# Up-projection of a two-layer-norm encoder trunk: a product form with four weight sums, accumulating PSUM banks and moved right-hand pools

## The chip, the cores and the metric

The kernel runs on one core of a Trainium2 chip. Its time is the device time of one execution in microseconds (us). The work is done by five engines that run side by side, each through its own queue of instructions in order: TensorE (PE, matrix products), VectorE (DVE), ScalarE (ACT), GpSimd (POOL) and SyncE (SP, which here only issues DMAs). Products are summed in PSUM, in eight banks of 512 fp32 columns per partition; all other tiles are in SBUF.

## What is computed

One layer with two sub-layers: token mixing (two attention branches and their merge) and a gated MLP with a causal convolution. The change touches the second, and the places where the first hands over to it:

```python
x = _layer_norm(alpha * x + (1.0 + g1) * mix, ln1_g[l], ln1_b[l])

h = _layer_norm(x) * (1.0 + sc2) + sh2
u = _causal_depthwise_conv(h @ w_up[l], conv_w[l], conv_b[l])   # width 3
a, val = jnp.split(u, 2, axis=-1)
y = (jax.nn.silu(a) * val) @ w_down[l]
x = _layer_norm(alpha * x + (1.0 + g2) * y, ln2_g[l], ln2_b[l])
```

S = 1024 rows, D_MODEL = 1024, D_FF = 2816; `h @ w_up` is 1024x1024 by 1024x5632.

## The kernel before

**Operands.** Every fp32 operand of a large product is split into a rounded high part and the rest (`hi`, `lo`, both fp32r), and a product of two is made of three matmuls: high by high, high by low, low by high (`mm3`). A "product" in the up-projection (`product`, L733) is 128 output channels by 512 rows with 512 of the contracted columns: 4 steps of k by 3 matmuls, 12 matmuls of 128x128 by 128x512, into one PSUM bank of the pool `mxp` (6 banks, tag "mm").

**Seven products for eight.** The 2816 gate channels a and the 2816 value channels go in 22 blocks c of 128. For one c the four weight parts are b12, b22 (value) and b11, b21 (gate), each 512x128, and h is cut into four parts h11, h12, h21, h22 of 512 by 512. Strassen's form takes seven products with sums of weights (`operand`, L723: an optional sum on DVE or POOL, a cast by ACT for the high part, a subtraction on POOL or DVE for the low part) and sums of h that are made once: `h_11`, `h_11p12` in the pool `ha` (left-hand side of SBUF) and `h_11p22`, `h_21p22`, `h_21m11`, `h_22`, `h_12m22` in the pool `hb` (right-hand side; tiles named hc0 to hc4 in the program). Each product has a bank of its own; ACT copies (L990, L992, L998) and eight DVE sums (L994 to L1007) join them in the single pair u of convolution inputs (uv the value half, ua the gate half). `conv` (L961) then runs on a PSUM tile `pcv`: ACT Identity (L963), two DVE multiply-adds (L965), and for the gate also silu on ACT (L968) and the product with the value half on DVE (L969). The result goes to DRAM.

**Order.** For c < 8 two of the seven products (of `h_11` and `h_11p12`) are made ahead (`ready`, `head`) and kept in DRAM (`md`): the heads 0 to 2 beside the second layer norm, 3 to 7 beside `turned_1`. The up-projection then alternates early blocks (five products left) with full ones: 0, 8, 1, 9, ... 7, 15, 16 ... 21. `raw` brings weights from DRAM by SP, 512 KB per half block; `slot` gives out ten tiles in turn for split weights.

**Stages, by time in the profile.** Attention until about 715 us; the merge of row half 0 (`merge`, products `psb` and then the mix `psm`) to 825; of half 1 beside the norms of half 0 to 872; `turned_0` (transposes h of half 0 and makes its operands) and the second mix to 959, with heads 0 to 2; `turned_1` (operands of half 1) with the heads 3 to 7 and the spreading of the row g2 (`psrow`) to 1007; the up-projection to 1392; the down-projection to the end. `put` (L867) makes one operand of h: an optional sum (L872), the high part (L874), the low part (L875), on three engines given by the call.

**Placement.** The pools `edge` (an unused tile, 32 bytes per partition), `wide`, the merge operands `oh`/`ol` and `hb` are on the right-hand side, so the size of `edge` sets where the others start.

## Time and profile before

| | |
|---|---|
| runs, us | 1648.75, 1640.61, 1645.29 |
| median, us | 1645.29 |
| the profiled execution's own time, us | 1646.35 |
| its span, first to last instruction, us | 1644.6 |
| mean granted TensorE clock | 0.981 of full |
| PE busy | 1566.4 us, 95% |
| DVE, ACT, POOL busy | 1144.6, 781.2, 560.1 us |

The span is what the trace shows; 1.75 us of the execution lie around it. A stage table (busy time of each engine in a stretch) tells which engine fills a stage, a list by line and shape gives counts and mean durations, and the timeline gives starts, from which the distance of two matmuls is read: a matmul's own duration overlaps the next.

### The profile page before, as it was taken

How to read it: one execution, taken by the hardware profiler on the slowest of the kernel's cores; microseconds unless marked ns; L12 is line 12 of the kernel's file. 1: busy time of each engine (PE TensorE's matmuls, PEld its weight loads, DVE VectorE, ACT ScalarE, POOL GpSimd, SP SyncE). 2: the span in 40 equal slices, each digit the busy share in tenths (PEclk: the TensorE clock that was granted, in tenths of full speed). 3: DMA queues.
4: the chain of work that ended last, by engine and by line, in shares of the span. 5: the costliest groups of instructions: out<-in, count | busy, mean ns of one | idle time of the engine just before them, and what ended most of it. 6: DMA issues, size and time to landing. Idle time of an engine off the chain costs nothing.

```text
span 1644.6 us, 22113 instructions
## 1 busy us (share of the span) xinstructions
PE 1566.4 (95%) x7821; PEld 1300.7 (79%) x7821; DVE 1144.6 (70%) x2293; ACT 781.2 (48%) x1382; POOL 560.1 (34%) x522
## 2 busy tenths in 40 slices
PE   6899999989999999999997979999999999999996
PEld 3787888879888888877875757888888888888885
DVE  6748776686677665537599786999998776544617
ACT  3447555655565556654235264544444444431311
POOL 1111213112222322222063756554455443650602
PEclk9999999999999999999998998999999999999998
DMA  9123432342152334246546244333322222851611
GB/s 346 45 85 121 145 92 70 120 129 65 65 179 78 103 103 123 71 150 236 166 154 230 96 166 160 115 110 122 129 102 90 77 71 90 270 197 39 204 39 52
DMA packets 81823, 205.81 MB, mean 125 GB/s; under 512 B 8560, under 2 KB 17328, under 8 KB 81712
## 3 DMA queue, kind: packets, MB, share of 16 engines
q1 hardware_dynamic: 77104, 197.49, 36.6%
q10 hardware_dynamic: 4608, 6.90, 1.1%
q8 instruction: 62, 1.02, 0.3%
q14 instruction: 49, 0.40, 0.1%
HBM read 157.14 MB, written 38.83 MB: 119 GB/s over the span
## 4 chain that ended last, share of the span: by engine, by line
PE 77%; DVE 13%; DMA 4%; ACT 2%; issue 2%; POOL 2%; DVEq 0%; SPq 0%; ACTq 0%; POOLq 0%
PE psu L213 8%; PE psu L212 8%; PE psu L211 8%; PE psd L1035 5%; PE psd L1033 5%; PE psd L1034 4%; PE pso L509 4%; PE psg L211 4%; PE psg L212 4%; PE psg L213 3%; PE pst L494 3%; PE psq L212 3%; PE psq L211 3%; PE psq L213 3%; PE psv L306 2%; PE psv L305 2%
## 5 line engine op out<-in xcount | busy, mean ns | idle before, releaser
L98 POOL TENSOR_TENSOR wl<-ws,wh 128x1024 fp32r<-128x1024 f32 x54 | 133.1, 2468 | 316.0 <-ACT wh L97 265.3
L1027 DVE TENSOR_TENSOR gl<-gs,gh 128x512 fp32r<-128x512 f32 x41 | 62.3, 1524 | 104.9 <-ACT gh L1026 100.2
L1033 PE MATMUL psd<-dd,gh 128*128 128x512 f32 x328 | 127.6, 389 | 0.0
L1034 PE MATMUL psd<-dd,gh 128*128 128x512 f32 x328 | 127.6, 389 | 0.0
L1035 PE MATMUL psd<-dd,gl 128*128 128x512 f32 x328 | 127.4, 389 | 0.0
L459 ACT ACTIVATE s<-s,mx 128x640 f32<-128x640 f32 (+7 forms) x128 | 94.6, 739 | 48.4 <-DVE mx L453 46.9
L498 ACT CAST pt<-pst 128x512 fp32r<-128x512 f32 (+1 forms) x192 | 82.4, 452 | 67.3 <-PE pst L494 63.4
L211 PE MATMUL psq<-h1h,wh 128*128 128x512 f32 x256 | 104.5, 410 | 0.4 <-DVE h1h L207 0.4
L211 PE MATMUL psu<-hc,wx 128*128 128x512 f32 x264 | 104.0, 394 | 0.0
L212 PE MATMUL psu<-hc,wx 128*128 128x512 f32 x264 | 104.0, 394 | 0.0
L213 PE MATMUL psu<-hc,wx 128*128 128x512 f32 x264 | 104.0, 394 | 0.0
L211 PE MATMUL psg<-h1h,wh 128*128 128x512 f32 x256 | 103.9, 406 | 0.0
L212 PE MATMUL psq<-h1l,wh 128*128 128x512 f32 x256 | 101.1, 395 | 1.8 <-DVE h1l L208 1.8
L213 PE MATMUL psq<-h1h,wl 128*128 128x512 f32 x256 | 101.0, 394 | 0.0
L499 DVE TENSOR_TENSOR pt<-pst,pt 128x512 fp32r<-128x512 f32 (+1 forms) x192 | 96.8, 518 | 5.9 <-ACT pt L498 4.0
L212 PE MATMUL psg<-h1l,wh 128*128 128x512 f32 x256 | 100.2, 392 | 0.0
L213 PE MATMUL psg<-h1h,wl 128*128 128x512 f32 x256 | 100.2, 391 | 0.0
L509 PE MATMUL pso<-pt,vs 128*128 128x256 f32 x608 | 92.1, 290 | 3.1 <-DVE o L514 1.7
L965 DVE SCALAR_TENSOR_TENSOR pcv<-u,convp,pcv 128x1024 f32<-128x1024 f32 x66 | 84.9, 1287 | 13.5 <-ACT pcv L963 12.6
L1021 POOL TENSOR_TENSOR dd<-ws,dd 128x1024 fp32r<-128x1024 f32 x25 | 62.2, 2490 | 89.1 <-ACT dd L1020 89.0
L509 PEld LDWEIGHTS pso<-pt,vs 128*128 128x128 f32 x608 | 81.8, 191 | 12.5 <-ACT pt L498 4.0
L963 ACT ACTIVATE pcv<-u,convp 128x1024 f32<-128x1024 f32 x44 | 53.2, 1210 | 76.0 <-DVE u L1007 31.4
(282 smaller groups left out, 4536.0 us busy)
## 6 DMA issues: line engine op xcount, KB each, us to landing
ws<-in_w_up SPq DMA_DIRECT2D x52, 512.0 KB, 3.7
wa<-in_w_ada SPq DMA_DIRECT2D x64, 256.0 KB, 3.0
ws<-in_w_down SPq DMA_DIRECT2D x28, 512.0 KB, 3.5
yd<-y SPq DMA_DIRECT2D x22, 512.0 KB, 2.6
gs<-yd SPq DMA_DIRECT2D x44, 256.0 KB, 3.7
wa<-in_w_ada SPq DMA_DIRECT2D x8, 1024.0 KB, 12.1
ws<-in_w_qk SPq DMA_DIRECT2D x16, 512.0 KB, 4.7
ws<-in_w_g SPq DMA_DIRECT2D x16, 512.0 KB, 3.8
```

Source lines behind the costliest of these rows:

```text
L98: po.tensor_sub(out=lo, in0=st, in1=hi)
L211: pe.matmul(ps, wh, xh, start=start, stop=False)
L212: pe.matmul(ps, wh, xl, start=False, stop=False)
L213: pe.matmul(ps, wl, xh, start=False, stop=stop)
L459: se.activation(out=st[:, 0:nk], in_=st[:, 0:nk], func=AF.Exp, scale=-1.0, bias=prev, accum_out=sm)
L498: se.copy(out=dh, in_=src)
L499: ve.tensor_sub(out=dl, in0=src, in1=dh)
L509: pe.matmul(ps[:, 0:256], vs[:, j0 + j, :], pt[c][j // 4][:, j % 4, :], start=j == 0 and c == 0, stop=j == nj - 1 and c == 1)
L965: ve.scalar_tensor_tensor(out=ps if d == 1 or b == 0 else y, in0=u[b][:, 2 - d : S + 2 - d], scalar=cp[:, 2 - d : 3 - d], in1=ps, op0=ALU. ...
L1033: pe.matmul(ps[n], g[0][:, ts], d[0][:, halves(n)], start=start, stop=False)
L1034: pe.matmul(ps[n], g[0][:, ts], d[1][:, halves(n)], start=False, stop=False)
L1035: pe.matmul(ps[n], g[1][:, ts], d[0][:, halves(n)], start=False, stop=stop)
```

## The change

The up-projection takes another seven-product form. Two sums follow from one another, s1 = w21 + w22 and s2 = s1 - w11, and two more are w12 - s2 and w11 - w21 (w11, w12 are the gate's parts, w21, w22 the value's); of h it takes h_11 and h_21 as they are (left-hand pool), and h_22, t1 = x - h11, t2 = y - t1, t3 = y - x, t4 = h21 - t2 (right-hand pool), where in the code x and y are the two column halves of the second row half. Products that end in the same output are added in PSUM: `main` takes w11 by h_11, then s2 by t2, (w11 - w21) by t3 and w22 by t4 on top of one another, `side` takes s1 by t1 and then (w12 - s2) by h_22; between two such products the bank is read off by an ACT copy or by a DVE sum. A sum of two such readings is all that is left of the joining. The number of products and of matmuls is the same. All low parts of the up-projection's weights are made on POOL. There are two pairs u in turn, the gate half is convolved first, and silu writes the SBUF tile y that the value half is multiplied into.

The heads are now w11 by h_11 and w12 by h_21, without a sum of weights; the second is added to the first by DVE instead of copied by ACT. `turned_0` casts h_21 without a sum. The unused tile `edge` grows from 32 to 96 bytes per partition, and in the built program every operand of the right-hand pools starts 64 bytes lower (modulo 128 bytes: before at 0, after at 64; the operand tiles of the left-hand pools are at 64 in both). The scratch for dynamic DMA shrinks from 16384 to 1024 bytes.

```diff
...
     edge = ctx.enter_context(tc.tile_pool(name="edge", bufs=1, side="right"))
-    po.memset(edge.tile([P, 8], F32, name="edge", tag="edge"), 0.0)
+    po.memset(edge.tile([P, 24], F32, name="edge", tag="edge"), 0.0)
 
...
     ha_cm, hap = opened(name="ha", bufs=1)
-    h_11, h_11p12 = operands(hap, "ha"), operands(hap, "hb")
+    h_11, h_21 = operands(hap, "ha"), operands(hap, "hb")
     mxp = ctx.enter_context(tc.tile_pool(name="mxp", bufs=6, space=PSUM, reuse_waits="tile"))
...
         if y is not None:
-            t = tmp.tile([P, 4, P], F32, name=nm("wt"), tag="ht", bufs=2 if tmp is mxb else 3)
+            t = tmp.tile([P, 4, P], F32, name=nm("wt"), tag="ht", bufs=2 if tmp is mxb else 4)
             eng.tensor_tensor(out=t, in0=x, in1=y, op=op)
...
 
-    def product(w, h):
-        ps = mxp.tile([P, H], F32, name=nm("psu"), tag="mm")
+    def product(w, h, ps=None):
+        on = ps is not None
+        if not on:
+            ps = mxp.tile([P, H], F32, name=nm("psu"), tag="mm")
         for k in range(4):
-            mm3(ps, w[:, 0, k, :], w[:, 1, k, :], h[k][0], h[k][1], k == 0, k == 3)
+            for a_, b_ in ((0, 0), (0, 1), (1, 0)):
+                first = k == 0 and (a_, b_) == (0, 0) and not on
+                pe.matmul(ps, w[:, a_, k, :], h[k][b_], start=first, stop=k == 3 and a_ == 1, skip_group_check=on)
         return ps
...
         if c < HEAD:
-            b12, b22 = raw(c, 1, wp, "ws")
+            w11, w12 = raw(c, 0, wp, "ws")
             raws.clear()
             lo = ve if c >= EARLY else po
-            readied.append((operand(head_slot, mxb, b12, b22, ALU.subtract, po, lo), operand(head_slot, mxb, b22, lo=lo)))
+            readied.append((operand(head_slot, mxb, w11, lo=lo), operand(head_slot, mxb, w12, lo=lo)))
 
     def head(c):
-        w3, w5 = readied.pop(0)
-        for i, ps in ((1, product(w3, h_11)), (0, product(w5, h_11p12))):
+        w11, w12 = readied.pop(0)
+        p1 = None
+        for i in range(2):
+            ps = product((w11, w12)[i], (h_11, h_21)[i])
             if c < EARLY:
...
                 t = hbp.tile([P, H], F32, name=nm("mc"), tag="mc", bufs=2)
-            se.copy(out=t, in_=ps)
+            if i == 0:
+                se.copy(out=t, in_=ps)
+                p1 = t
+            else:
+                ve.tensor_tensor(out=t, in0=ps, in1=p1, op=ALU.add)
             se.dma_start(out=md[c, i], in_=t)
...
             e[2].tensor_sub(out=dst[1], in0=x, in1=dst[0])
+            return x
 
...
                 put(h_11[j], x, e=(None, se, ve))
-                put(h_11p12[j], x, y, ALU.add, (ve, ve, po))
+                put(h_21[j], y, e=(None, ve, po))
 
...
             for j in range(4):
-                h11, h12 = [th.tile([P, H], F32, name=nm("hf"), tag="hf", bufs=4) for _ in range(2)]
+                h11, h21 = [th.tile([P, H], F32, name=nm("hf"), tag="hf", bufs=4) for _ in range(2)]
                 sy.dma_start(out=h11, in_=hx[j])
-                sy.dma_start(out=h12, in_=hx[j + 4])
+                sy.dma_start(out=h21, in_=hx[j + 4])
                 x, y = turned(tiles, j), turned(tiles, j + 4)
-                put(h_11p22[j], h11, y, ALU.add, (ve, se, po), th, 6)
-                put(h_21p22[j], x, y, ALU.add, (ve, se, po), th, 6)
-                put(h_21m11[j], x, h11, ALU.subtract, (ve, se, ve), th, 6)
                 put(h_22[j], y, e=(None, se, ve))
-                put(h_12m22[j], h12, y, ALU.subtract, (po, se, ve), th, 6)
+                t1 = put(h_t1[j], x, h11, ALU.subtract, (ve, se, po), th, 6)
+                t2 = put(h_t2[j], y, t1, ALU.subtract, (ve, se, po), th, 6)
+                put(h_t3[j], y, x, ALU.subtract, (po, se, ve), th, 6)
+                put(h_t4[j], h21, t2, ALU.subtract, (ve, se, ve), th, 6)
 
...
     hb_cm, hbp = opened(name="hb", bufs=1, side="right")
-    h_11p22, h_21p22, h_21m11, h_22, h_12m22 = [operands(hbp, f"hc{i}") for i in range(5)]
+    h_22, h_t1, h_t2, h_t3, h_t4 = [operands(hbp, f"hc{i}") for i in range(5)]
     th_cm, th = opened(name="th", bufs=2)
...
     fu_cm, fu = opened(name="fu", bufs=2)
-    u = [fu.tile([P, S + 2], F32, name=f"u{b}", tag=f"u{b}", bufs=1) for b in range(2)]
-    for b in range(2):
-        po.memset(u[b][:, 0:2], 0.0)
-    (ua0, ua1), (uv0, uv1) = [(u[b][:, 2 : H + 2], u[b][:, H + 2 : S + 2]) for b in range(2)]
+    us = [[fu.tile([P, S + 2], F32, name=f"u{i}{b}", tag=f"u{i}{b}", bufs=1) for b in range(2)] for i in range(2)]
+    for i in range(2):
+        for b in range(2):
+            po.memset(us[i][b][:, 0:2], 0.0)
+    turns = cycle(us)
+    def conv(c, b, y, u):
 
-    def conv(c, b, gate=None):
-        y = fu.tile([P, S], F32, name=nm("y"), tag=f"y{b}", bufs=2 - b)
         cp = convp[:, 2 * c + b, :]
...
         for d in (1, 2):
-            ve.scalar_tensor_tensor(out=ps if d == 1 or b == 0 else y, in0=u[b][:, 2 - d : S + 2 - d],
-                                    scalar=cp[:, 2 - d : 3 - d], in1=ps, op0=ALU.mult, op1=ALU.add)
+            ve.scalar_tensor_tensor(out=ps, in0=u[b][:, 2 - d : S + 2 - d], scalar=cp[:, 2 - d : 3 - d], in1=ps,
+                                    op0=ALU.mult, op1=ALU.add)
         if b == 0:
-            se.activation(out=ps, in_=ps, func=AF.Silu)
-            ve.tensor_tensor(out=y, in0=ps, in1=gate, op=ALU.mult)
-        return y
+            se.activation(out=y, in_=ps, func=AF.Silu)
+        else:
+            ve.tensor_tensor(out=y, in0=ps, in1=y, op=ALU.mult)
 
...
 
+    def add(out, x, y):
+        ve.tensor_tensor(out=out, in0=x, in1=y, op=ALU.add)
     def up(c):
-        b12, b22 = raw(c, 1, hbp, "fs")
-        b11, b21 = raw(c, 0, *((wp, "ws") if c not in order[:2] else (hbp, "fs")))
+        w21, w22 = raw(c, 1, hbp, "fs")
+        w11, w12 = raw(c, 0, *((wp, "ws") if c not in order[:2] else (hbp, "fs")))
         stored()
-        if c < HEAD:
-            sy.dma_start(out=uv0, in_=md[c, 0])
-            sy.dma_start(out=uv1, in_=md[c, 1])
+        u = next(turns)
+        (ua0, ua1), (uv0, uv1) = [(u[b][:, 2 : H + 2], u[b][:, H + 2 : S + 2]) for b in range(2)]
+        y = fu.tile([P, S], F32, name=nm("y"), tag="y", bufs=2)
+        early = c < HEAD
+        if early:
+            p1 = fu.tile([P, H], F32, name=nm("p1"), tag="p1", bufs=2)
+            sy.dma_start(out=p1, in_=md[c, 0])
+            sy.dma_start(out=ua0, in_=md[c, 1])
+        else:
+            main = product(operand(slot, ff, w11), h_11)
+            se.copy(out=ua0, in_=main)
+        s1 = ff.tile([P, 4, P], F32, name=nm("s1"), tag="ht", bufs=4)
+        ve.tensor_tensor(out=s1, in0=w21, in1=w22, op=ALU.add)
+        s2 = ff.tile([P, 4, P], F32, name=nm("s2"), tag="ht", bufs=4)
+        ve.tensor_tensor(out=s2, in0=s1, in1=w11, op=ALU.subtract)
+        if early:
+            main = product(operand(slot, ff, s2), h_t2)
+            add(ua1, main, p1)
+            side = product(operand(slot, ff, s1), h_t1)
+            add(uv1, side, p1)
+        else:
+            side = product(operand(slot, ff, s1), h_t1)
+            se.copy(out=uv1, in_=side)
+            product(operand(slot, ff, s2), h_t2, main)
+            se.copy(out=ua1, in_=main)
+        def third():
+            product(operand(slot, ff, w12, s2, ALU.subtract), h_22, side)
+            add(ua1, side, ua1)
+        if not early:
+            third()
+        product(operand(slot, ff, w11, w21, ALU.subtract), h_t3, main)
+        add(uv1, main, uv1)
+        if early:
+            third()
+        else:
+            m2 = product(operand(slot, ff, w12), h_21)
+            add(ua0, m2, ua0)
+        conv(c, 0, y, u)
+        product(operand(slot, ff, w22), h_t4, main)
+        if early:
+            add(uv0, main, p1)
         else:
-            m3 = product(operand(slot, ff, b12, b22, ALU.subtract), h_11)
-            se.copy(out=uv1, in_=m3)
-            m5 = product(operand(slot, ff, b22), h_11p12)
-            se.copy(out=uv0, in_=m5)
-        m1 = product(operand(slot, ff, b11, b22, ALU.add), h_11p22)
-        ve.tensor_sub(out=ua0, in0=m1, in1=uv0)
-        ve.tensor_tensor(out=uv0, in0=uv0, in1=uv1, op=ALU.add)
-        ve.tensor_tensor(out=uv1, in0=m1, in1=uv1, op=ALU.add)
-        m2 = product(operand(slot, ff, b11), h_21p22)
-        se.copy(out=ua1, in_=m2)
-        ve.tensor_sub(out=uv1, in0=uv1, in1=m2)
-        m6 = product(operand(slot, ff, b11, b12, ALU.add, po, ve), h_21m11)
-        ve.tensor_tensor(out=uv1, in0=m6, in1=uv1, op=ALU.add)
-        yv = conv(c, 1)
-        m4 = product(operand(slot, ff, b21, b11, ALU.subtract, po, ve), h_22)
-        ve.tensor_tensor(out=ua1, in0=m4, in1=ua1, op=ALU.add)
-        ve.tensor_tensor(out=ua0, in0=m4, in1=ua0, op=ALU.add)
-        m7 = product(operand(slot, ff, b21, b22, ALU.add), h_12m22)
-        ve.tensor_tensor(out=ua0, in0=m7, in1=ua0, op=ALU.add)
-        pending.append((c, conv(c, 0, yv)))
+            se.copy(out=uv0, in_=main)
+        conv(c, 1, y, u)
+        pending.append((c, y))
 
...
     arrays = {f"in_{k}": v for k, v in layout(inputs).items()}
-    nc = bacc.Bacc("TRN2", target_bir_lowering=False, num_devices=1)
+    nc = bacc.Bacc("TRN2", target_bir_lowering=False, num_devices=1, dynamic_dma_scratch_size=1024)
     aps = {
```

**DVE in `turned_0`, about 890 to 907 us.** `ht` is a sum of two h tiles, `hb` and `ha` are the operands, `wl` the low part of the second mix's weights (L109), for which the mix waits. Before:

```order
L872 TENSOR_TENSOR ht_9696<-h_2208_9683,h_2210_9690 128x512
L874 CAST hb_8498<-ht_9696 128x512
L875 TENSOR_TENSOR ha_8491<-h_2208_9683,ha_8490 128x512
L872 TENSOR_TENSOR ht_9718<-h_2213_9705,h_2215_9712 128x512
L874 CAST hb_8500<-ht_9718 128x512
L875 TENSOR_TENSOR ha_8493<-h_2213_9705,ha_8492 128x512
L872 TENSOR_TENSOR ht_9740<-h_2218_9727,h_2220_9734 128x512
L874 CAST hb_8502<-ht_9740 128x512
L875 TENSOR_TENSOR ha_8495<-h_2218_9727,ha_8494 128x512
L872 TENSOR_TENSOR ht_9762<-h_2223_9749,h_2225_9756 128x512
L874 CAST hb_8504<-ht_9762 128x512
L109 TENSOR_TENSOR wl_9841<-ws_9842,wh_9840 128x1024
```

After:

```order
L885 CAST hb_8498<-h_2210_9690 128x512
L886 TENSOR_TENSOR ha_8491<-h_2208_9683,ha_8490 128x512
L885 CAST hb_8500<-h_2214_9710 128x512
L886 TENSOR_TENSOR ha_8493<-h_2212_9703,ha_8492 128x512
L885 CAST hb_8502<-h_2218_9730 128x512
L886 TENSOR_TENSOR ha_8495<-h_2216_9723,ha_8494 128x512
L885 CAST hb_8504<-h_2222_9750 128x512
L886 TENSOR_TENSOR ha_8497<-h_2220_9743,ha_8496 128x512
L109 TENSOR_TENSOR wl_9833<-ws_9834,wh_9832 128x1024
L109 TENSOR_TENSOR wl_9864<-ws_9865,wh_9863 128x1024
```

Four sums of 128x512 (`ht`) are gone from the rows ahead of the mix's `wl`.

**ACT in a full block of the up-projection.** `psu` is a product's bank, `u` a half of a convolution input, `pcv` the convolution's PSUM tile, `wx`, `wh`, `wl` high parts of weights, `s` and `wt` weight sums. Before:

```order
L963 ACTIVATE pcv_11114<-u_10784,convp 128x1024
L729 CAST wx_11360<-wt_11361 128x512
L963 ACTIVATE pcv_11158<-u_10783,convp 128x1024
L990 COPY u_10784<-psu_11174 128x512
L729 CAST wx_11384<-wt_11385 128x512
L992 COPY u_10784<-psu_11191 128x512
L729 CAST wx_11404<-wt_11405 128x512
L968 ACTIVATE pcv_11158<-pcv_11158 128x1024
L729 CAST wh_11435<-wt_11436 128x512
L998 COPY u_10783<-psu_11229 128x512
```

After:

```order
L981 ACTIVATE y_11263<-pcv_11341 128x1024
L1013 COPY u_10761<-psu_11376 128x512
L976 ACTIVATE pcv_11362<-u_10760,convp 128x1024
L729 CAST wh_11571<-wt_11572 128x512
L1025 COPY u_10762<-psu_11397 128x512
L729 CAST wl_11594<-ws_11506 128x512
L1027 COPY u_10761<-psu_11376 128x512
L729 CAST wx_11621<-ws_11617 128x512
L729 CAST wx_11642<-s_2563_11638 128x512
L976 ACTIVATE pcv_11480<-u_10761,convp 128x1024
L1047 COPY u_10762<-psu_11376 128x512
```

The copies of `psu_11376` come three times, between products that add to this bank; before, each copy reads a bank that no later product of the block adds to.

**DVE at the beginning of the up-projection.** `u<-psu` rows read banks off, `wt` and `s` rows are sums of weights that wait for `ws` from DRAM, `mc` rows join a head. Before:

```order
L727 TENSOR_TENSOR wt_10873<-ws_10550,ws_10548 128x512
L727 TENSOR_TENSOR wt_10904<-ws_10898 128x512
L727 TENSOR_TENSOR wt_10940<-ws_10900,ws_10898 128x512
L994 TENSOR_TENSOR u_10783<-psu_10794,u_10784 128x512
L995 TENSOR_TENSOR u_10784<-u_10784 128x512
L996 TENSOR_TENSOR u_10784<-psu_10794,u_10784 128x512
L730 TENSOR_TENSOR wh_10978<-wt_10979,wh_10978 128x512
L727 TENSOR_TENSOR wt_11023<-ws_10900,ws_10898 128x512
L999 TENSOR_TENSOR u_10784<-u_10784,psu_10813 128x512
```

After:

```order
L1015 TENSOR_TENSOR s_2455_10894<-ws_10871 128x512
L770 TENSOR_TENSOR mc_10744<-psu_10731,mc_10728 128x512
L1017 TENSOR_TENSOR s_2456_10896<-s_2455_10894,ws_10873 128x512
L727 TENSOR_TENSOR wt_10932<-ws_10873,s_2456_10896 128x512
L995 TENSOR_TENSOR u_10759<-psu_10778,p_2436_10768 128x512
L727 TENSOR_TENSOR wt_10950<-ws_10873,ws_10871 128x512
L995 TENSOR_TENSOR u_10760<-psu_10795,p_2436_10768 128x512
L1015 TENSOR_TENSOR s_2473_11019<-ws_11010 128x512
L995 TENSOR_TENSOR u_10760<-psu_10778,u_10760 128x512
L1017 TENSOR_TENSOR s_2474_11021<-s_2473_11019,ws_11012 128x512
```

Rows of the weight sums of the next two blocks (`s_2455` to `s_2473`) now stand between the rows that read off the banks 10778 and 10795 of block 0, and two of the three readings are of banks to which a later product of the block is added.

## Rows read from the trace of the kernel before

**Rows 1.** First page: span; busy time, share of span and instruction count per engine.
```profile
span 1644.6 us, 22113 instructions
PE 1566.4 (95%) x7821; PEld 1300.7 (79%) x7821; DVE 1144.6 (70%) x2293; ACT 781.2 (48%) x1382; POOL 560.1 (34%) x522
```

**Rows 2.** Stage table: length, busy time (x instructions) per engine, PEclk, DMA share, GB/s.
```profile
715.00:825.00 110.00, 105.02 (x461) 85.13 (x460) 63.76 (x71) 41.27 (x47) 22.36 (x9) 0.98 0.58 195
825.00:872.00 47.00, 43.67 (x180) 34.34 (x179) 46.19 (x84) 18.66 (x24) 28.83 (x11) 0.96 0.51 175
872.00:903.00 31.00, 23.03 (x99) 17.22 (x97) 28.18 (x50) 19.81 (x26) 8.64 (x5) 0.83 0.66 234
903.00:959.00 56.00, 53.79 (x227) 43.19 (x228) 40.22 (x94) 21.87 (x34) 36.55 (x20) 0.97 0.35 122
959.00:1007.00 48.00, 35.28 (x152) 27.28 (x151) 36.32 (x38) 27.23 (x48) 27.59 (x21) 0.86 0.49 165
1007.00:1392.00 385.00, 385.00 (x1661) 310.36 (x1660) 323.29 (x382) 183.12 (x259) 192.05 (x140) 1.00 0.29 102
```

**Rows 3.** Timeline of PE, 1001 to 1010.5: start, duration, line, names; first matmuls of products.
```profile
1001.87 0.39 PE L211 MATMUL psu<-ha,wh 128*128 128x512 f32 x1
...
1004.59 0.39 PE L211 MATMUL psu<-hb,wl 128*128 128x512 f32 x1
...
1007.31 0.39 PE L211 MATMUL psu<-hc,wl 128*128 128x512 f32 x1
...
1010.11 0.39 PE L211 MATMUL psu<-hc,wx 128*128 128x512 f32 x1
```

**Rows 4.** Lines by shape, 1007 to 1392: count, busy, mean ns, idle before and releaser.
```profile
L211 PE MATMUL psu<-hc,wx 128*128 128x512 f32 x264 | 104.0, 394 | 0.0
L965 DVE SCALAR_TENSOR_TENSOR pcv<-u,convp,pcv 128x1024 f32<-128x1024 f32 x64 | 82.3, 1287 | 12.2 <-ACT pcv L963 11.3
L963 ACT ACTIVATE pcv<-u,convp 128x1024 f32<-128x1024 f32 x43 | 52.0, 1210 | 71.4 <-DVE u L1001 28.0 <-DVE u L1007 26.9 <-DVE y L965 15.7
L729 ACT CAST wx<-wt 128x512 fp32r<-128x512 f32 x61 | 37.6, 620 | 31.2 <-PE psu L213 30.8 <-DVE wt L727 0.2
L727 DVE TENSOR_TENSOR wt<-ws,ws 128x512 f32<-128x512 f32 x42 | 36.6, 871 | 17.4 <-POOL wx L730 10.2 <-POOL wh L730 4.2 <-POOL wl L730 2.6
L968 ACT ACTIVATE pcv<-pcv 128x1024 f32<-128x1024 f32 x21 | 21.2, 1008 | 21.1 <-DVE pcv L965 21.1
L999 DVE TENSOR_TENSOR u<-u,psu 128x512 f32<-128x512 f32 x22 | 15.2, 689 | 3.5 <-ACT u L998 1.5
L998 ACT COPY u<-psu 128x512 f32<-128x512 f32 x22 | 13.0, 589 | 21.7 <-PE psu L213 21.7
```

**Rows 5.** First page, DMA issues: engine, count, KB each, median us from issue to landing.
```profile
ws<-in_w_up SPq DMA_DIRECT2D x52, 512.0 KB, 3.7
```

**Rows 6.** Tile psb, 715 to 825: one matmul, ns min/median/max, first and last start.
```profile
L212 PE MATMUL psb<-ol,wh x65: 391/394/628, 728.9 to 824.8; 128*128 128x512 f32 x65
```

**Rows 7.** Timeline of DVE, 893 to 907: three of its four sums, then the mix's weights.
```profile
893.80 0.68 DVE L872 TENSOR_TENSOR ht<-h,h 128x512 f32<-128x512 f32 x1
...
895.47 1.78 DVE L872 TENSOR_TENSOR ht<-h,h 128x512 f32<-128x512 f32 x1
...
898.22 1.79 DVE L872 TENSOR_TENSOR ht<-h,h 128x512 f32<-128x512 f32 x1
...
901.97 4.50 DVE L109 TENSOR_TENSOR wl<-ws,wh 128x1024 fp32r<-128x1024 f32 x2
```

**Rows 8.** Timeline of PE, 900 to 909: idle before and its releaser in brackets.
```profile
904.31 0.69 PE L809 MATMUL psm<-wl,mh 128*128 128x512 f32 x1 [3.38 <-DVE wl L109]
...
905.23 0.63 PE L809 MATMUL psm<-wl,mh 128*128 128x512 f32 x1
905.65 0.63 PE L810 MATMUL psm<-wh,ml 128*128 128x512 f32 x1
```

**Rows 9.** Waits of PE over the whole span: total us, times, longest.
```profile
PE psrow L194 <- DVE gc L193: 16.2, 6, 5.6
```

## The prediction

> **What bounds the kernel now.** I read the first page for the shares of the engines [rows 1], then the stage table [rows 2], and only then went into stages, because the change touches three of them. The page alone says that PE is busy for 95% of the span. The stage table says where it isn't: in the up-projection (1007 to 1392 us) PE is busy 385.00 of 385 us at full clock, with DVE at 323.29, so this stage lasts exactly as long as its matmuls follow one another, and no saving on DVE, ACT or POOL can shorten it. In 872 to 903 PE is busy 23.03 of 31 us at 0.83 of the clock, in 959 to 1007 it is 35.28 of 48 at 0.86: there DVE is what PE waits for. In 825 to 872 DVE itself is full (46.19 of 47).
>
> In the full stage the only way to gain is a shorter distance between matmuls, and the timeline shows that there are two distances. A product is 12 matmuls. One that reads `ha` starts at 1001.87 and the next at 1004.59; one of `hb` goes from 1004.59 to 1007.31: 2.72 us each, 226.7 ns a matmul. The first product that reads `hc` goes from 1007.31 to 1010.11: 2.80 us, 233.3 ns [rows 3]. The mean duration of the hc matmuls, 394 ns over 264 of them, shows that this is not one product's accident [rows 4], since the records of `ha` and `hb` have 0.39 or 389. The merge's products `psb`, whose moving tiles lie on the right-hand side too, also have 394 as their median [rows 6].
>
> **The change part by part.** All terms are set against the profiled execution's 1646.35 us (span 1644.6 and 1.75 around it), which is 1.06 us above the median of the runs; that is taken off at the end.
>
> *The same number of matmuls.* Seven products a full block, five an early one, two a head, as before. So the new form gives PE neither more nor less to do; what can move is the distance of matmuls and the waits.
>
> *The right-hand pools, 64 bytes on.* `ha`, `hb` run at 226.7 ns and start at 64 modulo 128 bytes; `hc`, `oh`, `ol` run near 233.3 and start at 0. After the change all of them start at 64. If the start is the cause, the five hc products of each of 22 blocks gain 0.08 us each: 110 x 0.08 = 8.8 us, all of it on the path, since PE has no gap there. In the merge of half 0, where PE is busy 105.02 of 110 us [rows 2], 192 matmuls `psb` gain 6.7 ns each: 1.3 us. In that of half 1 DVE is the limit, and nothing is gained. Bounds: 0, if it is the side or the distance to the weights and not the start, and 10.1. I take 10.1, because the same operation with the same shapes differs in nothing else that I can see in the rows.
>
> *`turned_0` without four sums.* PE waits 3.38 us at 904.31 for the low part of the mix's weights, L109 [rows 8]. That DVE instruction starts at 901.97, straight behind a run of h operands, in which three sums take 0.68, 1.78 and 1.79 us [rows 7]. (The fourth is earlier and has a wait for a DMA behind it, so it is worth nothing.) Without them L109 starts up to 4.25 us earlier, which is more than the 3.38 of the wait. After the wait PE runs at the lower clock, the granted 0.83 of this stretch: matmuls at 905.23 and 905.65 are 0.42 apart [rows 8] instead of 0.227, for about eight of them, 1.6 us more. Together 5.0 us. Bounds: 1, if another input of the mix comes just behind (L109 on POOL, the transfers of w_out), and 6, if the next stretch profits too. I take 5.0: the named releaser is this instruction, and the sums stand straight ahead of it.
>
> *Heads.* Their weights need no sum any more, eight sums fewer on POOL, which no stage waits for. Their second product is now joined by DVE (0.69 us like L999 [rows 4]) instead of copied by ACT. Five such sums lie in 959 to 1007, where PE's longest list of waits is for `gc`, which DVE makes (16.2 us in six waits over the span, 5.6 the longest [rows 9]). Some of these sums stand ahead of a `gc`. Bounds 0 and 5 x 0.69 = 3.4; I take 1.0, since the last two come after the last `gc` and ones that fall in DVE's idle time cost nothing. `turned_1` has four sums for one j as before, three of them on DVE, but t2 now needs t1 and t4 needs t2: a chain of waits on DVE's own results, no extra instruction.
>
> *Products that add to a filled bank.* This is the new wait. Before, each product had a bank of its own of six, and PE could run ahead of the readers by some five products. Now a bank is read off by ACT or DVE between two products that add to it, and exactly one other product, 2.72 us, lies between. A copy takes 0.589 us (L998), a sum 0.69 (L999) [rows 4], so 2.1 and 2.0 us are left for whatever stands ahead in that engine's queue. A full block has four such re-entries, an early one three: 14 x 4 + 8 x 3 = 80. Ahead on ACT can stand an Identity of 1.21 and a cast of 0.62, 1.83 together: it fits. On DVE a multiply-add of 1.287 (L965) fits alone, and with a weight sum of 0.871 it is 2.16, over by a little. Following the queues of an early and a full block in turn (twelve products, 32.6 us, in which DVE has about 23 us to do) I find 1.1 to 1.9 us to spare at the tightest places. So in the steady state nothing, or a few tenths.
>
> At the beginning it is tighter. DVE's order has the weight sums of the next two blocks, which wait for `ws` from DRAM, ahead of sums that read off block 0's banks. A half block's weights take 3.7 us to land [rows 5], and their tile comes free only when the block before has been split (cast 0.620, low part on POOL). While DVE stands at such a sum, the reading behind it waits, and PE behind that. I work out two stalls of about 2.7 and 3 us there if the weights come as late as the tiles allow, and none if they come a block earlier. Bounds for the whole stage: 0 and 13 (these 6, and 0.9 in each of the eight pairs); I take 3.5, about half of the start's two stalls.
>
> *Edits costed at nothing.* Two pairs u, gate half first, silu into y: they loosen ACT and DVE, which PE doesn't wait for here; if that slack were gone, they would matter for the re-entries, and are counted there. All low parts on POOL: seven of 1.3 us a full block of 19 us, hidden by the ring of ten weight tiles. Smaller DMA scratch: the page lists hardware queues and instruction loads alone for the DMAs, so nothing here uses it that I can see.
>
> Sum: 1646.35 - 8.8 - 1.3 - 5.0 + 1.0 + 3.5 = 1635.75; less 1.06 for the median, **about 1635**.
>
> **The rivals.** About 0.5% (8.2 us) is what a measurement of this kernel can tell from no change: below 1637.1 is faster, above 1653.5 slower.
>
> *The start doesn't matter.* The 6.7 ns belong to the right-hand side, or to how far the tiles lie from something, and stay. For it: one group of transposes and narrow matmuls that start at several offsets shows no clear order. Against it: the matmuls are alike in all else. Then 1635 + 10.1 = 1645, no change. Of the skill's rules one speaks for this rival: in the Trainium skill, "TensorE: Matmul & The Clock Gate", section "Back-to-back issue gap", the distance of matmuls is given by the number of columns alone (518 cycles, about 216 ns, for 512), with no term for where an operand lies. By that rule the move gains nothing and the time is this rival's; the trace agrees on neither figure, with 226.7 and 233.3 ns for the same 512 columns [rows 3], so something beyond columns counts.
>
> *The gain in 872 to 1007 is used up.* DVE is the engine there before and after, and a PE that starts the mix earlier may only wait longer at `gc`. Then the 5.0 us go, and the time is 1640. For it: DVE has 28.18 of 31 and 36.32 of 48 us to do [rows 2]. Against: the sums are really gone and the mix is bound by PE right after (53.79 of 56).
>
> *Re-entries stall all along: the slower side.* If at most of the 80 re-entries the reading is behind by some tenths, PE loses that each time. With 2.16 us ahead on DVE against 2.0 left, or a second cast on ACT (2.45 against 2.1), it is 0.15 to 0.35 us. At 0.35 it is 28 us instead of the 3.5 taken: 1635 + 24.5, about 1660. It decides from (1653.5 - 1635 + 3.5) / 80 = 0.28 us a re-entry. For it: the single PSUM tile of the convolution ties ACT's Identity to DVE's progress, so a late DVE also holds ACT's copies. Against: the slack of 1.1 to 1.9 us above, and DVE loses four to six joins a block. One more rule bears on it: the Trainium skill, "Perfetto Trace Analysis", section "Matmul Optimizations", wants all eight PSUM banks used to have work in parallel, and the change goes the other way, from seven banks a full block to three. By it the stage would get waits like this rival's; the trace before, with a bank a product, has PE without any wait in this stage [rows 2], which fits the rule, but it doesn't show what fewer banks cost.
>
> **How the numbers follow.** Forecast (start matters, mix gains, re-entries cost little, 1627 to 1637): 0.58. Start doesn't matter (1645): 0.18. Gain used up (1640): 0.12. Re-entries stall (1660): 0.12. So faster by over 0.5%: 0.58, within: 0.18 + 0.12 = 0.30, slower: 0.12. The low end of the range is the sum with all gains, 6 in the mix and no stall, 1628, less a microsecond for heads that cost nothing; the high end takes in the second rival with stalls a little above those taken, 1648. The stalling rival is left out.
>
> **What would show it.** In the changed profile: products of all hc tiles 2.72 us apart and their mean near 389, and the up-projection's stretch about 376 to 380 us; PE's wait at the second mix below 1 us and no stretch of lower clock there; PE's list of waits with a few `psu` entries released by DVE sums at the beginning of the stage, 3 to 4 us in all. Wrong it would be if the hc distance stays 2.80, if the wait at the mix is only moved to `gc`, or if `psu` waits appear in every block.

## The result, and the profile after

| | before | changed |
|---|---|---|
| median, us | 1645.40 | 1649.99 |
| range of the runs, us | 1640.61 to 1648.75 | 1646.95 to 1654.18 |
| span of the profiled execution, us | 1644.6 | 1645.6 |
| DVE busy, us | 1144.6 | 1078.8 |

The ratio of the times is 1.0029 with a 95% interval of 1.0022 to 1.0036: 4.8 us more, which is inside the half per cent that was named as no change, and well away from the 1635 us that were forecast. 66 us of DVE's work are gone and the kernel is no faster.

The stage table of the changed kernel, to be laid beside [rows 2] (length, busy time and instructions of PE, PEld, DVE, ACT, POOL, then the granted clock, DMA share, GB/s):

```profile
872.00:903.00 31.00, 24.54 (x105) 18.99 (x106) 24.05 (x32) 18.89 (x25) 10.71 (x6) 0.83 0.70 247
903.00:959.00 56.00, 53.13 (x241) 42.90 (x240) 40.44 (x101) 24.31 (x37) 26.85 (x14) 1.00 0.41 144
959.00:1007.00 48.00, 36.87 (x142) 28.39 (x141) 35.41 (x42) 23.30 (x41) 24.84 (x21) 0.79 0.47 158
1007.00:1392.00 385.00, 381.03 (x1634) 307.26 (x1633) 255.72 (x270) 182.53 (x258) 182.22 (x138) 1.00 0.29 97
```

In the last row DVE has 255.72 us to do instead of 323.29, and PE, which had no gap there, now has gaps of 4.0 us in all, in two places. The lines of PE in that stage (busy us and mean ns of one, then idle time and releaser), beside [rows 4], say that the hc matmuls didn't become quicker:

```profile
L741 PE MATMUL psu<-hc,wx 128*128 128x512 f32 x801 | 194.2, 397 | 4.0 <-DVE u L995 4.0
L741 PE MATMUL psu<-hc,wl 128*128 128x512 f32 x262 | 64.6, 395 | 0.0
L741 PE MATMUL psu<-ha,wx 128*128 128x512 f32 x96 | 23.2, 390 | 0.0
```

The timeline of PE has the same in starts, beside [rows 3]: a product of `hb` (the left-hand h_21) and the product of `hc` behind it.

```profile
1103.27 2.90 PE L741 MATMUL psu<-hb,wh 128*128 128x512 f32 x12
1106.00 2.96 PE L741 MATMUL psu<-hc,wl 128*128 128x512 f32 x12
1108.79 1.56 PE L741 MATMUL psu<-hc,wx 128*128 128x512 f32 x6
```

2.73 us for the 12 matmuls of `hb`, 2.79 for those of `hc`. Inside the hc product the single matmuls are now 229 and 237 or 238 ns apart in turn, where they were 233 and 234 before: the shift by 64 bytes did something, but the mean stays at 233.2.

The second difference is the beginning of the stage. DVE and then PE in the changed kernel (start, duration, line; idle time before and its releaser in brackets):

```profile
1007.76 0.69 DVE L1017 TENSOR_TENSOR s<-s,ws 128x512 f32<-128x512 f32 x1 [4.60 <-DMA ws<-in_w_up]
1008.56 1.67 DVE L727 TENSOR_TENSOR wt<-ws,s 128x512 f32<-128x512 f32 x1
1010.15 0.68 DVE L995 TENSOR_TENSOR u<-psu,p 128x512 f32<-128x512 f32 x1
```

```profile
1005.00 2.97 PE L741 MATMUL psu<-hc,wx 128*128 128x512 f32 x12
1010.89 2.67 PE L741 MATMUL psu<-hc,wx 128*128 128x512 f32 x8 [2.92 <-DVE u L995]
```

DVE stands for 4.60 us at s2 of the second block, which waits for weights from DRAM, then makes one more weight sum, and only then reads off the bank of block 0's first product, which was complete at about 1005. PE wants to add to that bank at 1008.0 and waits 2.92 us. The chain of waits names what held the weights: a tile that came free only with the low parts of the block before.

```profile
1001.82 1.30 POOL wx L730
1003.12 1.27 POOL wh L730
1004.41 3.23 DMA ws<-in_w_up
1007.72 0.63 ACT wl L729
```

After the wait PE runs on at the lower clock level for a while (columns as in the stage table above, granted clock third from the end):

```profile
1010.80:1012.20 1.40, 1.31 (x6) 1.09 (x7) 1.40 (x3) 0.33 (x2) 1.40 (x2) 1.00 0.00 0
1012.20:1015.60 3.40, 3.40 (x10) 2.61 (x9) 0.32 (x1) 0.89 (x2) 3.40 (x4) 0.51 0.46 137
```

**Where the time went.** With the starts of matmuls as marks, the stages of this profile and of the experiments below are, in us (mix: first to last matmul of the second half of `psm`; heads: from head 3 to the up-projection; up: to the first product of the down-projection; down: to its last matmul):

| kernel | mix | heads 3 to 7 | up | down |
|---|---|---|---|---|
| before | 59.0 | 52.3 | 384.4 | 239.2 |
| changed | 54.9 | 54.2 | 390.6 | 239.1 |
| before, edge 224 bytes | 57.1 | 51.5 | 381.5 | 244.6 |
| changed, edge 224 bytes | 54.6 | 53.2 | 386.9 | 239.1 |
| changed, own banks | 53.7 | 53.4 | 384.3 | 239.1 |
| changed, own banks, edge 224 | 54.0 | 54.3 | 375.4 | 239.2 |

Over all kernels with the old form (seven profiles) the mix lasts 56.9 to 59.0 us, mean 57.9, and the heads 51.0 to 52.5, mean 51.7; over those with the new form the mix lasts 53.4 to 55.9, mean 54.4 (seven profiles), and the heads 53.2 to 54.4, mean 53.9 (six, without the one that changes them). So the new form gains 3.5 in the mix, loses 2.2 in the heads and 6.1 in the up-projection: 4.8 us more, which is what the runs show. That it agrees to a tenth is luck, since the up-projection is taken from one profile of each kernel. Single profiles differ by some five us in the attention (its end lies between 723.9 and 729.1) and in the first merge and mix, which the change hardly touches; differences between two spans are therefore not read here, only stages.

### The profile page after: what moved, and what is told of

The parts are those of the page before. It is cut to its first block, busy times and chain, and to the rows that moved or that the text cites. A ratio compares the mean times of both kernels' runs of the same rounds, so it can differ in the third digit from the quotient of the medians.

```text
span 1645.6 us, 21971 instructions
## 1 busy us (share of the span) xinstructions
PE 1564.6 (95%) x7821; PEld 1301.3 (79%) x7821; DVE 1078.8 (66%) x2189; ACT 780.1 (47%) x1380; POOL 540.5 (33%) x516
## 5 line engine op out<-in xcount | busy, mean ns | idle before, releaser
L741 PE MATMUL psu<-hc,wx 128*128 128x512 f32 x804 | 194.9, 397 | 4.0 <-DVE u L995 4.0
L741 PEld LDWEIGHTS psu<-hc,wx 128*128 128x128 f32 x804 | 151.9, 189 | 41.4 <-DVE u L995 4.8
L978 DVE SCALAR_TENSOR_TENSOR pcv<-u,convp,pcv 128x1024 f32<-128x1024 f32 x88 | 113.0, 1284 | 48.2 <-ACT pcv L976 47.6
L97 ACT CAST wh<-ws 128x1024 fp32r<-128x1024 f32 x54 | 56.4, 1047 | 67.6 <-PE psq L212 20.6
L494 PE MATMUL pst<-ident,s 128*128 128x128 f32 x528 | 81.7, 273 | 7.1 <-DVE pt L499 3.7
```

Source lines behind the costliest of these rows:

```text
L741: pe.matmul(ps, w[:, a_, k, :], h[k][b_], start=first, stop=k == 3 and a_ == 1, skip_group_check=on)
L978: ve.scalar_tensor_tensor(out=ps, in0=u[b][:, 2 - d : S + 2 - d], scalar=cp[:, 2 - d : 3 - d], in1=ps, op0=ALU.mult, op1=ALU.add)
```

## Experiments

The disputed step was the 64 bytes. First the edge tile alone, in both kernels.

**The changed value in the kernel before.**

```diff
-    po.memset(edge.tile([P, 8], F32, name="edge", tag="edge"), 0.0)
+    po.memset(edge.tile([P, 24], F32, name="edge", tag="edge"), 0.0)
```

> The kernel before with the edge tile of 96 bytes alone (right-hand operands from 0 to 64 modulo 128, which is from 256 to 192 modulo 512). The prediction's step, start modulo 128 decides: products of hc 2.72 us, time 10 us less, 1635. Theory now, the place modulo 512 against the left-hand tiles' 64 decides: the hc matmuls keep a mean of 233 ns, now as 229 and 238 in turn as in the changed kernel, time within 2 us of before. Rival, the right-hand side as such costs: 233 as well, so this run alone doesn't tell these two apart.

Measured: ratio to before 0.9992 (0.9982 to 1.0003), up-projection 384.2 us, hc matmuls 229 and 238 ns apart in turn, mean 233.3; their mean duration is 395.

```profile
L212 PE MATMUL psu<-hc,wx 128*128 128x512 f32 x263 | 103.8, 395 | 0.0
```

The step as the prediction made it has fallen: a start of 64 modulo 128 gives nothing.

**The kernel before, 192 bytes further.**

```diff
-    po.memset(edge.tile([P, 8], F32, name="edge", tag="edge"), 0.0)
+    po.memset(edge.tile([P, 56], F32, name="edge", tag="edge"), 0.0)
...
-    nc = bacc.Bacc("TRN2", target_bir_lowering=False, num_devices=1)
+    nc = bacc.Bacc("TRN2", target_bir_lowering=False, num_devices=1, dynamic_dma_scratch_size=1024)
```

> The kernel before with an edge tile of 224 bytes, by which the right-hand operands start at 64 modulo 512 like those of the left-hand side, and with the small DMA scratch, which makes room for it. Theory, place modulo 512: hc matmuls 226.7 ns apart, up-projection 375.5 us instead of 384.4, merge of half 0 1.3 us shorter, in all about 10 us less, 1635. Rival, right-hand side as such: 233 ns, time as before, 1645.

Measured: the matmuls are 226.7 ns apart, all 1305 of them at 226 or 227, but the time is not 10 us less: ratio 1.0013 (0.9999 to 1.0027). Lines and waits (total us, times, longest) of PE in the up-projection and behind it:

```profile
L211 PE MATMUL psu<-hc,wx 128*128 128x512 f32 x264 | 102.7, 389 | 0.0
...
PE psu L211 <- DVE u L996: 4.8, 4, 1.4
PE psd L1033 <- DVE u L1005: 3.4, 1, 3.4
```

Half of the expectation came true and the other half showed a limit that the old form had just behind PE. The waits come at the end, in the full blocks, at one place in each:

```profile
1306.31 0.50 PE L211 MATMUL psu<-hb,wx 128*128 128x512 f32 x1 [1.39 <-DVE u L996]
1327.04 0.50 PE L211 MATMUL psu<-hb,wx 128*128 128x512 f32 x1 [1.38 <-DVE u L996]
1347.77 0.50 PE L211 MATMUL psu<-hb,wl 128*128 128x512 f32 x1 [1.39 <-DVE u L996]
```

The last three are 20.73 us apart, while a block's matmuls take 7 x 2.72 = 19.0. The reading is that 20.7 us is what a full block takes in the old form by the joining and the convolution through one pair u; at 233 ns the matmuls took 19.4, and PE's lead of six banks hid the rest for the six full blocks at the end. No run gave the old form a second pair, so this cause is argued. With faster matmuls the lead is used up; the up-projection gains 2.9 us instead of 8.8, and the down-projection, whose first products need a bank that the last block still holds, loses 5.5 (3.4 of waiting, the rest of it matmuls at the lower clock behind the wait).

**The changed kernel with the old edge, and with one of 224 bytes.**

> The changed kernel with the old edge of 32 bytes (right-hand operands at 256 modulo 512). If the 64 bytes move nothing, hc at 233.3 without the alternation and the time within 2 us of the changed kernel, 1650. If they cost something by themselves, less.

> The changed kernel with an edge of 224 bytes (right-hand operands at 64 modulo 512). Theory, place modulo 512: hc matmuls 226.7 ns apart, about 10 us less than the changed kernel, 1640, if the re-entries into filled banks still fit into a product of 2.72 instead of 2.80 us; if they don't, psu waits appear in the later blocks and the gain is some us smaller. Rival, right-hand side as such: 233 ns and 1650.

Measured for the old edge: ratio to before 1.0033 (1.0017 to 1.0049), hc at 233.3, up-projection 392.3: the change of 64 bytes is worth nothing that can be measured here either. For 224 bytes: 0.9995 (0.9983 to 1.0007), 1644.2 us, that is 5.8 us less than the changed kernel instead of 10; the up-projection takes 386.9. The matmuls have 226.9 ns, but the waits have grown, from 4.0 in two places to 7.9 in six:

```profile
PE psu L741 <- DVE u L995: 4.9, 3, 3.4
PE psu L741 <- ACT u L1013: 3.0, 3, 1.0
```

The second row is new beside the changed kernel: an ACT copy that reads off `main` of a full block comes 1 us late three times.

**A bank for each product, in the new form.** The algebra, the weight sums, the two pairs u and the order of the products stay; no product is added to a filled bank. For a full block (early blocks in the same way):

```diff
-            se.copy(out=uv1, in_=side)
-            product(operand(slot, ff, s2), h_t2, main)
-            se.copy(out=ua1, in_=main)
+            add(uv0, product(operand(slot, ff, s2), h_t2), ua0)
+            add(ua1, side, uv0)
...
-        product(operand(slot, ff, w11, w21, ALU.subtract), h_t3, main)
-        add(uv1, main, uv1)
+        main = product(operand(slot, ff, w11, w21, ALU.subtract), h_t3)
+        add(uv1, main, ua1)
+        add(uv0, main, uv0)
...
-        product(operand(slot, ff, w22), h_t4, main)
-            se.copy(out=uv0, in_=main)
+        add(uv0, product(operand(slot, ff, w22), h_t4), uv0)
```

> The changed kernel, but every product of the up-projection in a bank of its own, as before the change: nothing is added to a filled bank, and DVE joins the seven banks of a full block in seven sums instead of three sums and four ACT copies. The rest (four weight sums, two pairs u, edge of 96 bytes) stays. Theory: the up-projection's 6.1 us over before come from PE standing at re-entries behind a DVE that waits for weights from DRAM; without re-entries the stage is 384 to 385 us, no psu wait is left in it, and the time is 6 us less than the changed kernel, 1644. Rival, the weights themselves arrive late for PE at the beginning: the wait of about 3 us near 1008 stays, only with a weight tile as what PE waits for, and the time stays at 1649 to 1650.

> The same with an edge of 224 bytes, so that all matmuls of the stage are 226.7 ns apart. Theory: the two gains add, since two pairs u leave DVE and ACT room in a full block (the old form with one pair needed 20.7 us a full block, PE needs 19.05): stage 375.5 to 377 us, time about 15 us less than the changed kernel, 1635. Rival, seven sums a block make DVE the limit as in the old form: psu waits in the full blocks at the end, stage 381, 1640.

Measured: with the edge of 96 bytes 0.9987 (0.9972 to 1.0001), 1643.4 us, and 384.3 in the up-projection; with 224 bytes 0.9925 (0.9904 to 0.9945), **1632.6 us**, and 375.4 there. The stage rows of the two, and the hc matmuls of the second:

```profile
1001.00:1386.00 385.00, 385.00 (x1660) 311.36 (x1660) 290.29 (x335) 161.69 (x219) 189.30 (x141) 1.00 0.28 100
```

```profile
1006.00:1382.00 376.00, 376.00 (x1661) 311.33 (x1660) 286.96 (x335) 159.47 (x217) 191.20 (x141) 1.00 0.29 103
...
L741 PE MATMUL psu<-hc,wx 128*128 128x512 f32 x800 | 186.9, 389 | 0.0
```

PE has no gap in either. That settles the 6.1 us: weights that arrive late were not what PE lacked (the rival), since the same transfers are late here too, as DVE's rows in the kernel with 96 bytes show:

```profile
1006.17 0.69 DVE L1017 TENSOR_TENSOR s<-s,ws 128x512 f32<-128x512 f32 x1 [3.70 <-DMA ws<-in_w_up]
1006.97 1.70 DVE L727 TENSOR_TENSOR wt<-ws,s 128x512 f32<-128x512 f32 x1
1008.59 0.68 DVE L995 TENSOR_TENSOR u<-psu,p 128x512 f32<-128x512 f32 x1
```

It was the reading that stood behind them, and it matters only where a later product of the block needs the bank. (The edit also turns the four ACT copies of a full block into DVE sums; the two long waits that it removes were both for a DVE sum.) DVE does 31 us more than in the changed kernel for it, 287 of 376, and PE has no wait from it. And it shows what the new form is worth: with the same 226.7 ns the old form stopped at 381.5 and 244.6, the new one, with two pairs u and fewer sums, gives 375.4 and 239.2; which of the two differences does it, no run separates.

**Bringing the second block's weights earlier instead**, banks added to as in the changed kernel, edge of 224 bytes:

```diff
-        w11, w12 = raw(c, 0, *((wp, "ws") if c not in order[:2] else (hbp, "fs")))
+        w11, w12 = raw(c, 0, *((wp, "ws") if c not in order[:1] else (hbp, "fs")))
```

> The changed kernel with an edge of 224 bytes and the second block's gate weights brought into the pool of the heads' weights, whose tiles come free earlier; banks are added to as in the changed kernel. Theory: DVE's sum of weights for the second block waited for that transfer and held the reading of block 0's bank; with the transfer earlier the stalls near 1008 and 1038 go, stage 378 to 380, about 13 us less than the changed kernel, 1637. Rival, the wait moves to the next block's weights, which then stand ahead of the reading: a stall of 2 to 4 us stays near 1010 and the time is 1642 to 1644.

Measured: 0.9974 (0.9959 to 0.9989), 1640.3 us, 385.2 in the stage. The mechanism is the rival's; the time lies between the theory's 1637 and the rival's 1642 to 1644. DVE no longer stands at s2 of the second block but at s1 of the third, and that one too has its place ahead of the reading:

```profile
1004.62 1.10 DVE L1015 TENSOR_TENSOR s<-ws 128x512 f32<-128x512 f32 x1 [2.50 <-DMA ws<-in_w_up]
1005.81 1.58 DVE L1017 TENSOR_TENSOR s<-s,ws 128x512 f32<-128x512 f32 x1
1007.31 0.68 DVE L995 TENSOR_TENSOR u<-psu,p 128x512 f32<-128x512 f32 x1
```

PE's wait there is 3.7 us instead of 3.4 in the kernel with the same edge. In all PE waits 6.9 us in the stage instead of 7.9.

**What the place means.** Three variants of the kernel before with the small scratch: 192 bytes more at the beginning of the left-hand side, so that left and right both start at 256 modulo 512, and two more edges (tiles of 160 and of 480 bytes per partition). Each ran once (1647.1, 1647.1 and 1648.3 us), so only the distances of matmuls are read from them, not the times.

```diff
     const = ctx.enter_context(tc.tile_pool(name="const", bufs=1))
+    po.memset(const.tile([P, 48], F32, name="lpad", tag="lpad"), 0.0)
```

> The kernel before with 192 bytes more at the beginning of the left-hand side (and the small DMA scratch): now all tiles of split weights and operands, left and right, start at 256 modulo 512. Theory a, only the moving operand's own start counts, and 64 is good: the matmuls of ha, hb and of the down-projection's dd go from 226.7 to 233 ns and hc stays there, about 10 us slower. Theory b, the moving operand's start against the stationary one's counts: all of them run at 226.7, hc too, and the down-projection keeps 226.7.

> The kernel before with the small scratch and an edge of 160 bytes: right-hand operands at 128 modulo 512, 64 bytes off the left-hand tiles' 64. It maps the distance between the moving operand's start and the stationary one's. So far 0 gives 226.7, 128 gives 229 and 238 in turn, 192 gives 233.3. Expected by theory: a mean of about 233 again, with or without alternation; if only distances of 128 and more cost, 226.7.

> The kernel before with the small scratch and an edge of 480 bytes: right-hand operands at 320 modulo 512, which is 256 off the left-hand tiles' 64. If the place counts modulo 512, about 233; if it counts modulo 256, 226.7.

In the first, the hc matmuls are 226.7 ns apart although they start where they did before the change, and the down-projection's `dd`, moved by 192 bytes together with its stationary tiles, keeps 226.7 (the rows give the mean durations, 389 ns):

```profile
L212 PE MATMUL psu<-hc,wx 128*128 128x512 f32 x264 | 102.7, 389 | 0.0
...
L1035 PE MATMUL psd<-dd,gh 128*128 128x512 f32 x325 | 126.4, 389 | 0.0
```

So it is not where the moving operand starts but how far its start lies from that of the stationary operand. The distances between starts in the up-projection, over the roughly 1300 pairs of hc matmuls of each profile (the starts are those of the built programs, as in the expectations; a profile has no addresses, only the steps between the runs follow from the edits):

| right start minus left start, modulo 512 bytes | hc matmuls, ns apart | from |
|---|---|---|
| 0 | 226.7 | left moved; edge 224 bytes |
| 64 | 229.1 (225 to 237) | edge 160 |
| 128 | 233.2 (229 and 238 in turn) | edge 96, as in the change |
| 192 | 233.3 (233 and 234) | before |
| 256 | 226.7 | edge 480 |

A distance of 256 is as good as 0, so in this one pair the place counts modulo 256. The expectation for 64 bytes was too high, 233 instead of 229.

**The scratch alone.**

> The kernel before with the small DMA scratch alone. It moves the left-hand pools 15360 bytes down, a multiple of 512, and frees room that nothing uses. Theory: no effect, hc at 233.3 ns, time within 2 us of before. Rival: the scratch or the place has a part in the changes seen with it, and the time moves by more than 3 us.

Ratio 1.0001 (0.9990 to 1.0012): no effect.

**The heads' joins.** From the kernel with own banks and the edge of 224 bytes:

```diff
-            if i == 0:
-                se.copy(out=t, in_=ps)
-                p1 = t
-            else:
-                ve.tensor_tensor(out=t, in0=ps, in1=p1, op=ALU.add)
+            se.copy(out=t, in_=ps)
...
+            add(ua0, ua0, p1)
             add(uv0, product(operand(slot, ff, s2), h_t2), p1)
```

> The kernel with a bank for each product and the edge of 224 bytes, but the heads' second product is copied by ACT again and joined later, by a sum of two SBUF tiles in the up-projection's early blocks (eight DVE sums of 0.7 to 1.7 us there). It takes DVE's joins out of the stage with the heads 3 to 7, which in the changed kernel is 2 us longer than before. Theory a, those joins stand ahead of what PE waits for: the stage from head 3 to the up-projection falls from 54.2 to about 52 us and the time by 2 us. Theory b, the chain t1, t2, t4 of sums makes the stage longer: it stays at 54 and the time is the same within 1 us.

Measured: 0.9932 (0.9918 to 0.9946), 1634.4 us. The stage of the heads falls from 54.3 to 52.5 us, as theory a has it, but the time doesn't fall: the up-projection grows from 375.4 to 377.1, with a wait that wasn't there:

```profile
PE psu L741 <- DVE u L990: 1.1, 1, 1.1
```

So in this one profile the 2 us of the heads go with the joins, and moved to the next stage they are paid there. Whether the chain of t1, t2 and t4 costs something beside that isn't settled: in this kernel the stage is 0.8 us above the mean of the old form, which is no more than single profiles differ by.

## Why the prediction was wrong, step by step

- **What bounds the kernel.** Right, and it is why 66 us less on DVE bring nothing: in the up-projection PE alone counts, and the old form had no gap to close.
- **The right-hand pools: the step that failed**, 10.1 us of the 10.6 that the sum came to. It read from [rows 3, 4] that the place of the tiles decides, and so far it was right: with an edge of 224 bytes the predicted 226.7 ns are there. But it took the moving tile's own start for the cause, and it is the distance to the start of the stationary one: with the left-hand side moved, hc gains the 6.6 ns from its old start. It then took 64 modulo 128 for the good place because that is where the left-hand tiles stand, without asking for the place modulo a larger number. They stand at 64 modulo 512, the right-hand ones went from 256 to 192, and the distance between the two, 192 or 128 modulo 256, costs the same 6.6 ns. The bound 0 was named, with the distance to the weights as a reason for it; taking the upper end rested on one pair of places, from which neither this nor a modulus can be told.
- **The merge's 1.3 us.** Wrong as well: `psb` stays at 232.8 ns on average, and there is another reason. Where `psb` does run at 227 ns (seven profiles) the first merge and mix last 97.0 us on average, where it runs at 229 to 233 (seven profiles) 96.3. So shorter distances gain nothing that shows there, though PE is busy for 105 of 110 us; single profiles differ by up to 5 us in this stage, and what sets its length stays open.
- **`turned_0`.** Mechanism right, size 3.5 instead of 5.0. The wait of 3.38 us in the mix [rows 8] is 0.22 now, with the granted clock at 1.00 instead of 0.97 in the stretch behind it. The first row shows what is left of it, the second that DVE now begins the low parts at 896.62 instead of 901.97 [rows 7]. Of these 5.35 us, 2.8 are only that the mix as a whole began earlier in this profile (876.4 instead of 879.3): measured from there, L109 starts 2.5 us earlier, not up to 4.25, and its bracket names what holds it now, a cast by ACT.

```profile
898.51 0.50 PE L820 MATMUL psm<-wl,mh 128*128 128x512 f32 x1 [0.22 <-DVE wl L109]
```

```profile
896.62 2.97 DVE L109 TENSOR_TENSOR wl<-ws,wh 128x1024 fp32r<-128x1024 f32 x2 [0.40 <-ACT wh L108]
```

- **The heads.** Sign right, size 2.2 instead of 1.0, inside the bounds; the wait was wrong. The joins were to stand ahead of `gc`, but PE's waits for `gc` in this stage are much shorter now (first row before, second row changed):

```profile
L194 PE MATMUL psrow<-ident,gc 128*128 128x128 f32 x16 | 3.7, 340 | 12.6 <-DVE gc L193 12.6
L194 PE MATMUL psrow<-ident,gc 128*128 128x128 f32 x16 | 3.9, 333 | 3.7 <-DVE gc L193 3.7
```

Waits for ACT have come in their place (3.9 us for `h`, 3.4 for `wl`), and all of PE's waits in the stage sum to 13.4 before and 13.3 after. What grew is PE's busy time, at a lower granted clock (before, changed, then own banks with the joins moved):

```profile
955.00:1007.30 52.30, 38.93 (x169) 29.99 (x168) 38.56 (x49) 31.47 (x53) 28.01 (x21) 0.87 0.52 173
948.00:1002.20 54.20, 40.87 (x169) 31.60 (x168) 42.08 (x65) 31.20 (x53) 22.77 (x20) 0.81 0.55 181
950.20:1002.70 52.50, 38.25 (x169) 28.43 (x168) 39.22 (x53) 32.93 (x56) 22.43 (x19) 0.87 0.54 185
```

With the joins moved the clock is back at 0.87 and the stage at 52.5 us, so by one profile the joins are the likely cause; how they bring the clock down isn't shown.
- **Products added to a filled bank.** Place and mechanism right, DVE standing at weight sums ahead of a reading; 6.1 us instead of 3.5. The two waits sum to 4.0; the rest, about 2, is matmuls at the lower clock, nearly all behind the first of them (granted 0.51 from 1012.2 to 1015.6), a cost that I had counted for the wait in `turned_0` and forgot here. In the steady state no wait is left behind 1039, but with products of 2.80 us. The 1.1 to 1.9 us to spare were worked out for 2.72, and at that length they weren't there: the changed kernel with the edge of 224 bytes has three waits of 1.0 us behind ACT's copy, at 1063, 1097 and 1228.
- **The rivals.** The time came out near the first one, "the start doesn't matter": 1645 with the stalls as taken, 1648 with them as measured, and 1650 with mix and heads as measured too. But it did so for a reason that lies between it and the forecast: the start matters, and the change moves it to a place that is no better. The issue-gap rule weighed there (the Trainium skill, "TensorE: Matmul & The Clock Gate", "Back-to-back issue gap") gave the right sign for this change, since nothing came of the move; the kernel with own banks and the edge of 224 bytes, with the same 512 columns and 9 us less in the stage than with 96 bytes, shows that the gap has a term for the place all the same. Of the second rival a part came true: of 3.5 us gained in the mix the heads lost 2.2. The third didn't in this kernel, where PE waits at two re-entries. The other rule, all eight banks in use (the Trainium skill, "Perfetto Trace Analysis", "Matmul Optimizations"), agrees in its direction: own banks are worth the 6.2 us between 390.6 and 384.3. The pool has six banks in both kernels, though, so no run here shows what the number of banks is worth.
- **The range** ended at 1648 and should have held the first rival with its upper bound of stalls, 1645 and 9.5 more. Two slips in the working changed nothing: by its own terms the low end is 1630 and 1629, not 1628 and 1627, and DVE loses five joins in a full block and three in an early one (eight before, three and five after), not four to six.

## What to carry to other kernels

When the same matmul runs at two speeds, note the addresses of both operands modulo several powers of two before choosing one, and try two shifts, not one. Where PE reads off and adds to the same bank, look at what stands ahead of the reading in DVE's and ACT's queues, above all instructions that wait for a transfer; here a bank for each product removed all of these waits, an earlier transfer only some, and no run changed the order in DVE's queue. And when the bound is moved, look for the limit just behind it: the faster matmuls were worth nothing in the old form, 6 us in the changed one and 9 us of the up-projection with own banks; the changed form cost 5 us by itself, and only with banks of their own do both pay, 0.75% together.

## What the runs showed of the hardware

That a matmul's distance to the next depends on how the start of its moving operand lies to that of its stationary one, modulo 256 bytes: 226.7 ns at 0, 229.1 at 64, 233.2 at 128, 233.3 at 192, for 512 fp32r columns at full clock. No run tells which part of the engine or the memory makes it. The figure for 64, and a run at 256 that gave 226.7 like 0, are one profile each. And in the changed kernel one wait of 2.92 us was followed by some 3.4 us at a granted clock of 0.51, so that it cost 4.9 in all (the distances of the matmuls there, less 233 ns each).
